# A squared-ReLU MLP's first matrix by a seven-product scheme: high and low rows of the stationary activations side by side in matmuls of 512 columns, two of four weight sums made by accumulating loads

## The chip, the cores and the metric

The kernel runs on one core of a Trainium2 chip. The metric is the device time of one launch in microseconds. The core's engines are TensorE (PE in the profile, its weight loads PEld), VectorE (DVE), ScalarE (ACT), GpSimd (POOL) and SyncE (SP, which here only issues DMAs). Each engine takes its instructions in its own fixed order; semaphores make it wait for others.

## What is computed

One layer of a hybrid decoder on 512 tokens, with 16 learned meta tokens ahead of them, all in float32: D_MODEL is 2048, D_FF 8192.

```python
u = rmsnorm(h, norm_mix[l])
proj = u @ w_in[l]
...
mix = jnp.concatenate([att.astype(x.dtype), hm], axis=-1)
h = h + mix @ w_out[l]
u = rmsnorm(h, norm_mlp[l])
h = h + jnp.square(jax.nn.relu(u @ w_up[l])) @ w_down[l]
```

The left-out part is a sliding-window attention with sinks and an mLSTM, both read from `proj` and concatenated. The change lies in `u @ w_up[l]`, which with its Relu and square is a matrix of 512 x 8192 results, each a sum over 2048.

## The kernel before

**Numbers.** A float32 product is made of three faster ones. `split` turns a tile into a high part, a cast to fp32r by ScalarE (L124), and a low part, source minus high part by VectorE (L125). Then high x high, high x low and low x high go into the same PSUM bank. Splitting a weight tile of 128 x 1024 takes one such pair of instructions; `hi_lo` gives the two result tiles, three pairs deep.

**Stages.** In order of time: w_in with attention and mLSTM, w_out (`tok_gemm`, L715 to L717), w_up (`up_quad`), w_down (L1104 to L1108). All four are matrix products against weights that stream in from DRAM once.

**w_up.** It is a Strassen-Winograd scheme: D_MODEL, D_FF and the tokens are each cut in halves or pairs, so that a block of results of 2 x 2 parts takes seven products in place of eight, at the price of sums of weights, of activations and of results. There are 32 quads (`NQ`), each of 256 columns of w_up: x11, x12, x21, x22 are its four weight parts of 128 x 1024 (eight k-tiles side by side), which come in two tiles `raws[0]` (x11, x12) and `raws[1]` (x22, x21) by two loads of 1 MB on SP's queue. Even quads use the two-deep pool of `raw_tile`, odd quads two tiles of their own, so four are there in all. The activations' operands y, seven pairs of high and low tiles, are split once and stay in SBUF.

The products p run in the order 0, 1, 5, 4, 6, 2, 3. The weight operands are x11, x12, s2, s1, s3, s4, x22, with s1 = x21 + x22, s2 = s1 - x11, s3 = x11 - x21, s4 = x12 - s2, all made by VectorE (`w_sum`, L753). A product is 8 k-tiles of three matmuls of 256 columns (L784: high weights on high rows, L785: high on low, L786: low on high), in which the weights are the 128 x 128 side that is loaded and the rows of y stream. Some of the sums over products are done in PSUM (a later product goes on in the bank X or Q without a start), the others by VectorE (L839, L848, L851) on copies that ScalarE made (L837, L840 and others). Results stand in `d` (two deep), which ScalarE takes through Relu (L849, L852, L853) and Square (L854). VectorE makes four more sums `fs` of d for w_down's own seven-product scheme (L857 to L860). Both go to DRAM by DMAs on ScalarE's queue (L861, L862).

**Quad 0** is different: its products lie between the last pieces of w_out, and its seven results stand in banks until VectorE joins them (L819 to L823).

**GpSimd** meanwhile does a job of its own: from quad 6 to 21 of the source, one unit of the residual `hd` a quad, in two halves; each half is a load into `res`, a product by a scalar and a store back (L1014, L1015, L1018). `res` is one tile, so each step waits for the last one. In w_down GpSimd issues the accumulating stores into `hd` (L1114).

**Order.** A tile framework's scheduler decides in which order each engine takes its instructions, from the program's order and from its own estimate of times; buffers come from pools, and an allocation waits for the release of the tile that had the place before.

## Time and profile before

| what | value |
|---|---|
| time, median of 3 runs | 1968.13 us (1967.82 to 1968.39) |
| the profiled execution's own time | 1967.29 us |
| its span in the trace | 1965.5 us |
| TensorE clock granted over the span | 0.998 |
| PE / VectorE / ScalarE / GpSimd busy | 99% / 71% / 51% / 12% |
| the w_up stage behind quad 0 | 733.5 to 1344.6 us |

The page gives busy times over the whole span; its slices of the span show PE at 9 tenths or more in all but the last one of 40, VectorE at 7 to 8 tenths from about 690 us on, and the DMA engines at 4 to 5 tenths in the w_up stage and 6 to 8 tenths in w_down. Instructions are listed with their line, the tile that they write and those that they read. A row of the list in order of time is: start, duration, engine, line, operation, and in brackets the idle time of the engine before it with what ended that. A row of the groups is: line, engine, operation, tiles, count, then busy time and mean duration in ns, then idle time before. PE busy is no sign of a limit by itself, as matmuls are pipelined: their durations overlap, and the distance of their starts is what one costs.

### The profile page before, as it was taken

The numbers are of one execution on the slowest core, as the hardware profiler recorded it, in microseconds if no ns is written. First come the engines' busy times: TensorE is split into PE (matmuls) and PEld (weight loads), VectorE is DVE, ScalarE is ACT, GpSimd is POOL, SyncE is SP. The second block draws the span as 40 slices with busy tenths as digits, with TensorE's granted clock in tenths as the row PEclk, the third lists the DMA queues.
The fourth block names the chain that finished last, engine by engine and source line by source line (L and its number), as shares of the span: only waits on it lengthen the run. The fifth ranks groups of instructions, "written<-read, shape, count | busy, mean of one in ns | idle before, by whom it ended". The sixth has DMA issues, their size and how long they took to land.

```text
span 1965.5 us, 30627 instructions
## 1 busy us (share of the span) xinstructions
PE 1948.6 (99%) x12240; PEld 1745.1 (89%) x12240; DVE 1405.3 (71%) x1843; ACT 1011.3 (51%) x1491; POOL 233.9 (12%) x346
## 2 busy tenths in 40 slices
PE   9999999999999999999999999999999999999997
PEld 7878889988888899999999999998888888888886
DVE  5547773233644378787878787878888988888888
ACT  4433542245533255555555555556566566655655
POOL 0112220011211001222222000001100010010001
PEclk9999999999999999999999999999999999999999
DMA  8412112221243335555555454547888887788866
GB/s 315 136 65 88 65 64 72 90 77 65 85 169 130 131 132 182 189 193 180 196 177 199 153 172 150 172 162 249 212 224 214 231 223 214 223 206 211 216 178 195
DMA packets 112752, 324.61 MB, mean 165 GB/s; under 512 B 14016, under 2 KB 50496, under 8 KB 93648
## 3 DMA queue, kind: packets, MB, share of 16 engines
q1 hardware_dynamic: 66880, 247.65, 36.9%
q0 software_dynamic: 12320, 41.95, 11.0%
q10 hardware_dynamic: 33408, 33.04, 5.3%
q8 instruction: 96, 1.57, 0.3%
q14 instruction: 48, 0.39, 0.1%
HBM read 244.45 MB, written 78.15 MB: 164 GB/s over the span
## 4 chain that ended last, share of the span: by engine, by line
PE 95%; DVE 2%; ACT 1%; issue 1%; POOL 0%; DMA 0%; DVEq 0%; ACTq 0%; POOLq 0%
PE g L171 10%; PE X L1107 6%; PE X L1108 6%; PE X L1104 6%; PE g L784 5%; PE g L786 5%; PE g L785 5%; PE a L784 5%; PE a L786 5%; PE a L785 5%; PE g L716 3%; PE g L715 3%; PE g L717 3%; PE Q L1107 3%; PE Q L1108 3%; PE Q L1104 3%
## 5 line engine op out<-in xcount | busy, mean ns | idle before, releaser
L124 ACT CAST whi<-raw 128x1024 fp32r<-128x1024 f32 x223 | 234.2, 1050 | 403.8 <-PE g L717 85.5
L125 DVE TENSOR_TENSOR wlo<-raw,whi 128x1024 fp32r<-128x1024 f32 x223 | 273.2, 1225 | 202.4 <-ACT whi L124 197.4
L125 DVE TENSOR_TENSOR wlo<-s,whi 128x1024 fp32r<-128x1024 f32 x255 | 311.9, 1224 | 108.2 <-ACT whi L124 106.9
L124 ACT CAST whi<-s 128x1024 fp32r<-128x1024 f32 x255 | 267.8, 1051 | 198.6 <-PE g L785 61.0
L171 PE MATMUL g<-s,whi 128*128 128x264 f32 x1216 | 205.0, 287 | 0.2 <-DVE qa L270 0.2
L171 PEld LDWEIGHTS g<-s,whi 128*128 128x128 f32 x1216 | 170.9, 189 | 5.4 <-issue 4.9
L1107 PE MATMUL X<-wlo,s 128*128 128x512 f32 x348 | 135.5, 389 | 0.1
L1108 PE MATMUL X<-whi,s 128*128 128x512 f32 x348 | 135.4, 389 | 0.0
L1104 PE MATMUL X<-whi,s 128*128 128x512 f32 x348 | 135.4, 389 | 0.0
L171 PE MATMUL g<-s,wlo 128*128 128x264 f32 x608 | 128.0, 287 | 0.0
L784 PE MATMUL a<-y,whi 128*128 128x256 f32 x448 | 125.6, 281 | 0.7 <-DVE d L839 0.7
L786 PE MATMUL a<-y,wlo 128*128 128x256 f32 x448 | 125.4, 280 | 0.6 <-DVE wlo L125 0.6
L785 PE MATMUL a<-s,whi 128*128 128x256 f32 x448 | 125.4, 280 | 0.0
L786 PE MATMUL a<-s,wlo 128*128 128x256 f32 x448 | 125.2, 279 | 0.0
L785 PE MATMUL a<-y,whi 128*128 128x256 f32 x448 | 125.2, 280 | 0.0
L784 PE MATMUL a<-s,whi 128*128 128x256 f32 x448 | 125.1, 279 | 0.0
L784 PE MATMUL g<-y,whi 128*128 128x256 f32 x444 | 124.6, 281 | 0.0
L785 PE MATMUL g<-s,whi 128*128 128x256 f32 x444 | 124.2, 280 | 0.0
L786 PE MATMUL g<-y,wlo 128*128 128x256 f32 x444 | 124.2, 280 | 0.0
L785 PE MATMUL g<-y,whi 128*128 128x256 f32 x444 | 124.1, 280 | 0.0
L786 PE MATMUL g<-s,wlo 128*128 128x256 f32 x444 | 124.0, 279 | 0.0
L784 PE MATMUL g<-s,whi 128*128 128x256 f32 x444 | 123.8, 279 | 0.0
(385 smaller groups left out, 5114.3 us busy)
## 6 DMA issues: line engine op xcount, KB each, us to landing
raw<-in_w_dram SPq DMA_DIRECT2D x144, 1024.0 KB, 5.1
rh<-in_w_dram SPq DMA_DIRECT2D x64, 512.0 KB, 5.6
hd<-c POOLq DMA_DIRECT2D x61, 512.0 KB, 5.6
fu<-fd SPq DMA_DIRECT2D x108, 256.0 KB, 3.9
fd<-d ACTq DMA_DIRECT2D x32, 512.0 KB, 3.2
fd<-fs ACTq DMA_DIRECT2D x31, 512.0 KB, 3.5
xtok<-in_x_dram SPq DMA_DIRECT2D x4, 1024.0 KB, 11.5
hs<-in_x_dram SPq DMA_DIRECT2D x16, 256.0 KB, 5.8
```

The lines of the kernel that those rows point to most:

```text
L124: act.copy(dst_hi, src)
L125: dve.tensor_tensor(out=dst_lo, in0=src, in1=dst_hi.bitcast(F32), op=ALU.subtract)
L171: pe.matmul(ps[s], w, x[:, PARTS[s]], start=first and kt == 0, stop=last and kt == KT - 1,)
L715: pe.matmul(ps[b][:], a, wh, start=kt == first, stop=False)
L716: pe.matmul(ps[b][:], a, wl, start=False, stop=False)
L717: pe.matmul(ps[b][:], c, wh, start=False, stop=kt == last)
L784: pe.matmul(out, wh, ah_, start=start and q == 0, stop=False, skip_group_check=True)
L785: pe.matmul(out, wh, al_, start=False, stop=False, skip_group_check=True)
L786: pe.matmul(out, wl, ah_, start=False, stop=q == KQ - 1, skip_group_check=True)
L1104: pe.matmul(out[:, t], a, wh[:, cols], start=start and h == q == 0, stop=False, skip_group_check=True)
L1107: pe.matmul(out[:, t], a, wl[:, cols], start=False, stop=False, skip_group_check=True)
L1108: pe.matmul(out[:, t], a2, wh[:, cols], start=False, stop=h == q == 1, skip_group_check=True)
```

## The change

**Rows.** The high and low rows of y are stored anew: for every k-tile the 256 high columns and right behind them the 256 low ones (`y_pair`, with `yy` the row of 512). In quads 1 to 31 a k-tile is now a matmul of 512 columns (high weights on the row) and one of 256 (low weights on the high half), in place of three of 256. PE's list of matmuls goes from 12096 to 10360 in the program. High x high and high x low thus come out in two halves of a whole bank and must be added: X, W and Q are banks of 512 columns now, `e` holds copies and PSUM sums of 512 columns (`accumulate`), and `join` adds the halves into `d`. Quad 0 keeps its matmuls of 256.

**Sums.** With signs turned, the operands are x11, x12, x11 + x21 + x22, x21 + x22, x11 + x21, x12 + x11 + x21 + x22, x22. Two sums are made by loads: `s0` gets x21 by a third load on SP and x11 on top of it by an accumulating load on GpSimd's queue; x21 gets x22 on top in the same way. VectorE makes the other two in place (x11 += x21, x12 += x11). The activations' sums turn signs to match, and the results' Relu becomes two instructions on alternate quarters of `d`, one with scale +1 and one with -1.

**Buffers.** Sum tiles go from three to two, `d` from two to one, the tile `shift` goes, `e` (128 x 2048 float32) comes, and both raw tiles are taken before the first load.

```diff
@@ -40,7 +40,7 @@
 QB = 2
 NQ = FF // P // 2
 HTOK = SEQ // 2
-NS_ = 3
+NS_ = 2
 FB = 5
 MAN = {mybir.EngineType.PE}
 ORDER = (0, 1, 5, 4, 6, 2, 3)
@@ -722,14 +722,15 @@
     b2s = ExitStack()
     b2 = b2s.enter_context(tc.tile_pool(name="b2", bufs=1, reuse_waits="tile"))
-    yh, yl = {}, {}
+    yy, yh, yl = {}, {}, {}
     def y_pair(p, j, t):
-        o = 16 * (j // 2)
-        yh[p, j], yl[p, j] = (t[:, o + i * 512 : o + (i + 1) * 512].rearrange("p (q n) -> p q n", q=2) for i in range(2))
-    b2.tile([P, 16], F32, name="shift")
+        o = 32 * (j // 3)
+        rows = t[:, o : o + 1024]
+        yy[p, j] = rows.rearrange("p (q m) -> p q m", q=2)
+        yh[p, j], yl[p, j] = (rows.rearrange("p (q a n) -> p a q n", q=2, a=2)[:, i] for i in range(2))
     for p in ORDER:
         for j in range(2):
             y_pair(p, j, b2.tile([P, 1024], F32R, name=f"y{p}_{j}"))
@@ -755,18 +756,19 @@
     done, summed = {}, {}
     def up_quad(quad):
-        raws = []
+        raws = [b2r.tile([P, 2048], F32, name=f"raw{i}") if quad % 2 else raw_tile() for i in range(2)]
         for i in range(2):
-            if quad % 2:
-                raw = b2r.tile([P, 2048], F32, name=f"raw{i}")
-            else:
-                raw = raw_tile()
-            load = sync.dma_start(out=raw[:], in_=io["w3"][quad, i])
+            load = sync.dma_start(out=raws[i][:], in_=io["w3"][quad, i])
             if quad == 2:
                 tc.keep_in_program_order(load)
-            raws.append(raw)
         x11, x12 = raws[0][:, :1024], raws[0][:, 1024:]
         x22, x21 = raws[1][:, :1024], raws[1][:, 1024:]
+        s0 = sum_tile()
+        if quad > 0:
+            sync.dma_start(out=s0[:], in_=io["w3"][quad, 1, :, 1024:])
+            pool.dma_start(out=s0[:], in_=io["w3"][quad, 0, :, :1024], accum_op=ALU.add)
+            pool.dma_start(out=x21, in_=io["w3"][quad, 1, :, :1024], accum_op=ALU.add)
         if quad == NQ - 1:
             u = sum_tile()
@@ -774,26 +776,32 @@
                 k = len(loaded)
                 loaded[k] = u[:, h * 512 : (h + 1) * 512]
                 load_unit(k, loaded[k])
-        s1, s2, s3, s4 = (sum_tile() for _ in range(4))
         nb = abank if quad % 2 else bank
-        def product(p, w, out, q0=0, q1=KQ, start=True):
-            for q in range(q0, q1):
-                wh, wl = (t[:, q * P : (q + 1) * P] for t in w)
-                ah_, al_ = yh[p, q // 2][:, q % 2], yl[p, q // 2][:, q % 2]
-                pe.matmul(out, wh, ah_, start=start and q == 0, stop=False, skip_group_check=True)
-                pe.matmul(out, wh, al_, start=False, stop=False, skip_group_check=True)
-                pe.matmul(out, wl, ah_, start=False, stop=q == KQ - 1, skip_group_check=True)
+        def relu(d, i):
+            r = d.rearrange("p (a b) n -> p b a n", a=2)[:, i]
+            act.activation(r, r, AF.Relu, scale=(1.0, -1.0)[i])
         if quad == 0:
...
             pa, pb, pc = (nb((P, 2, HTOK)) for _ in range(3))
             pd = nb((P, HTOK))
             pp2, pp6 = pd[:], pa[:, 1]
-            w_sum(s1, x21, x22, ALU.add)
-            w_sum(s2, s1[:], x11, ALU.subtract)
-            w_sum(s4, x12, s2[:], ALU.subtract)
-            early = [(p, operand(src), o) for p, src, o in ((0, x11, pa[:, 0]), (1, x12, pp2), (2, s4[:], pc[:, 1]))]
-            op4 = slot_operand(s1[:])
+            w_sum(s0, x21, x22, ALU.add)
+            w_sum(x21, x21, x11, ALU.add)
+            op0, op1 = operand(x11), operand(x12)
+            w_sum(x11, x11, s0[:], ALU.add)
+            w_sum(x12, x12, x11, ALU.add)
+            early = [(0, op0, pa[:, 0]), (1, op1, pp2), (2, operand(x12), pc[:, 1])]
+            op4 = slot_operand(s0[:])
             yield
             product(*early[0], 0, 2)
             yield
@@ -808,11 +816,10 @@
             product(4, op4, pb[:, 1])
             dve.tensor_tensor(out=w[1][:], in0=x22, in1=w[0][:].bitcast(F32), op=ALU.subtract)
             product(3, w, pc[:, 0])
-            w_sum(s3, x11, x21, ALU.subtract)
-            product(6, operand(s3[:]), pb[:, 0])
-            product(5, operand(s2[:]), pp6)
-            d = b2b.tile([P, 4, HTOK], F32, name="d", bufs=2)
+            product(6, operand(x21), pb[:, 0])
+            product(5, operand(x11), pp6)
+            d = b2b.tile([P, 4, HTOK], F32, name="d")
             v = b2b.tile([P, 4, HTOK], F32, name="fs")
             sb, u2, u = v[:, 2], v[:, 3], v[:, :2]
             act.copy(sb, pa[:, 0])
@@ -821,36 +828,49 @@
             dve.tensor_tensor(out=u, in0=v[:, 3:].to_broadcast([P, 2, HTOK]), in1=pb[:], op=ALU.add)
             dve.tensor_tensor(out=d[:, 3], in0=u[:, 0], in1=pb[:, 1], op=ALU.add)
             dve.tensor_tensor(out=d[:, 1:3], in0=u, in1=pc[:], op=ALU.add)
-            act.activation(d[:], d[:], AF.Relu)
         else:
-            X, B = nb((P, HTOK)), nb((P, 2, HTOK))
-            W, Q = B[:, 0], B[:, 1]
-            d = b2b.tile([P, 4, HTOK], F32, name="d", bufs=2)
-            product(0, operand(x11), X[:])
-            act.copy(d[:, 0], X[:])
-            w_sum(s1, x21, x22, ALU.add)
-            w_sum(s2, s1[:], x11, ALU.subtract)
+            def product(p, w, out, start=True):
+                for q in range(KQ):
+                    wh, wl = (t[:, q * P : (q + 1) * P] for t in w)
+                    row = yy[p, q // 2][:, q % 2]
+                    pe.matmul(out[:], wh, row, start=start and q == 0, stop=False, skip_group_check=True)
+                    pe.matmul(out[:, :HTOK], wl, row[:, :HTOK], start=False, stop=q == KQ - 1, skip_group_check=True)
+            def accumulate(dst, src, bank):
+                dve.tensor_tensor(out=dst, in0=src, in1=bank[:], op=ALU.add)
+            def join(d, e):
+                dve.tensor_tensor(out=d, in0=e[..., :HTOK], in1=e[..., HTOK:], op=ALU.add)
+            X, W, Q = (nb() for _ in range(3))
+            e = b2b.tile([P, 4, 512], F32, name="e")
+            d = b2b.tile([P, 4, HTOK], F32, name="d")
+            product(0, operand(x11), X)
+            act.copy(e[:, 0], X[:])
             product(1, operand(x12), W)
+            w_sum(x11, x11, x21, ALU.add)
             if quad == NQ - 1:
                 for k in (2, 3):
                     split_unit(k, loaded[k])
-            product(5, operand(s2[:]), X[:], start=False)
-            dve.tensor_tensor(out=d[:, 0], in0=d[:, 0], in1=W, op=ALU.add)
-            act.copy(d[:, 2], X[:])
-            product(4, operand(s1[:]), Q)
-            w_sum(s3, x11, x21, ALU.subtract)
-            act.copy(d[:, 1], Q)
-            product(6, operand(s3[:]), X[:], start=False)
-            w_sum(s4, x12, s2[:], ALU.subtract)
-            act.copy(d[:, 3], X[:])
-            product(2, operand(s4[:]), Q, start=False)
-            dve.tensor_tensor(out=d[:, 3], in0=d[:, 3], in1=d[:, 1], op=ALU.add)
-            act.activation(d[:, 0], d[:, 0], AF.Relu)
-            product(3, operand(x22), X[:], start=False)
-            dve.tensor_tensor(out=d[:, 2], in0=d[:, 2], in1=Q, op=ALU.add)
-            act.activation(d[:, 2:4], d[:, 2:4], AF.Relu)
-            act.activation(d[:, 1], X[:], AF.Relu)
+            product(5, operand(x11), X, start=False)
+            accumulate(e[:, 0], e[:, 0], W)
+            act.copy(e[:, 2], X[:])
+            product(4, operand(x21), Q)
+            act.copy(e[:, 1], Q[:])
+            join(d[:, 0], e[:, 0])
+            product(6, operand(s0[:]), X, start=False)
+            w_sum(x12, x12, x11, ALU.add)
+            accumulate(e[:, 3], e[:, 1], X)
+            product(2, operand(x12), Q, start=False)
+            accumulate(e[:, 2], e[:, 2], Q)
+            product(3, operand(x22), X, start=False)
+            join(d[:, 2:4], e[:, 2:4])
+            act.copy(e[:, 1], X[:])
+            join(d[:, 1], e[:, 1])
+        relu(d[:], 0)
+        relu(d[:], 1)
         done[quad] = act.activation(d[:], d[:], AF.Square)
         fs = b2b.tile([P, 4, HTOK], F32, name="fs")
         summer = dve if quad < NQ - 1 else pool
@@ -931,9 +951,10 @@
             split(yh[0, j][:], yl[0, j][:], y11)
             split(yh[1, j][:], yl[1, j][:], y21)
             split(yh[2, j][:], yl[2, j][:], y22)
-            dve.tensor_tensor(out=t1, in0=y12, in1=y11, op=ALU.subtract)
-            dve.tensor_tensor(out=t2, in0=y22, in1=t1, op=ALU.subtract)
-            dve.tensor_tensor(out=t4, in0=y21, in1=t2, op=ALU.subtract)
+            dve.tensor_tensor(out=t1, in0=y11, in1=y12, op=ALU.subtract)
+            dve.scalar_tensor_tensor(out=t2, in0=y22, scalar=-1.0, in1=t1, op0=ALU.mult, op1=ALU.subtract)
+            dve.scalar_tensor_tensor(out=t4, in0=t2, scalar=-1.0, in1=y21, op0=ALU.mult, op1=ALU.subtract)
             dve.tensor_tensor(out=t3, in0=y22, in1=y12, op=ALU.subtract)
             for p, src in ((4, t1), (3, t4), (6, t3), (5, t2)):
                 split(yh[p, j][:], yl[p, j][:], src)
```

The places in the order, first VectorE between quad 0 and quad 1. Names: `fs_66..` and `g_63..` are quad 0's results, `d_6613` its output, raw0 and raw1 quad 1's weights, wlo the low half of an operand; L125 is the subtraction of `split`. Before:

```order
L125 TENSOR_TENSOR wlo_6642<-raw0_6630,whi_6641 128x1024
L125 TENSOR_TENSOR wlo_6673<-raw0_6630,whi_6672 128x1024
L819 TENSOR_TENSOR d_6613<-fs_6614,g_6349 128x256
L820 TENSOR_TENSOR fs_6614<-fs_6614,g_6346 128x256
L753 TENSOR_TENSOR s_6634<-raw1_6632 128x1024
L821 TENSOR_TENSOR fs_6614<-fs_6614,g_6347 128x512
```

After, at the same place (`d_6609` is quad 0's output, `raw0_6627` quad 1's first tile):

```order
L826 TENSOR_TENSOR d_6609<-fs_6610,g_6345 128x256
L827 TENSOR_TENSOR fs_6610<-fs_6610,g_6342 128x256
L828 TENSOR_TENSOR fs_6610<-fs_6610,g_6343 128x512
L125 TENSOR_TENSOR wlo_6641<-raw0_6627,whi_6640 128x1024
L829 TENSOR_TENSOR d_6609<-fs_6610,g_6343 128x256
L830 TENSOR_TENSOR d_6609<-fs_6610,g_6344 128x512
L125 TENSOR_TENSOR wlo_6662<-raw0_6627,whi_6661 128x1024
L877 TENSOR_TENSOR fs_6620<-d_6609 128x256
L879 TENSOR_TENSOR fs_6620<-d_6609 128x256
L878 TENSOR_TENSOR fs_6620<-fs_6620,d_6609 128x256
L880 TENSOR_TENSOR fs_6620<-d_6609,fs_6620 128x256
L754 TENSOR_TENSOR raw0_6627<-raw0_6627,raw1_6628 128x1024
```

Both low halves of quad 1's first products stood ahead of quad 0's result sums; now three of those stand ahead of the first low half, five ahead of the second, and quad 0's four fs sums stand ahead of quad 1's first weight sum.

Second, GpSimd's queue in the middle of w_up, the residual loop. Two halves of it before:

```order
L1014 DMA res_9920<-hd2_0_5097 128x256
L1015 TENSOR_SCALAR res_9920<-res_9920,i2_6500 128x256
L1018 DMA hd2_0_5097<-res_9920 128x256
L1014 DMA res_9924<-hd2_0_5097 128x256
L1015 TENSOR_SCALAR res_9924<-res_9924,i2_6500 128x256
L1018 DMA hd2_0_5097<-res_9924 128x256
```

The same two halves after (`s_8807` and `raw1_8804` are s0 and x21 of a coming quad):

```order
L1035 DMA res_9161<-hd2_0_5097 128x256
L1036 TENSOR_SCALAR res_9161<-res_9161,i2_6497 128x256
L1039 DMA hd2_0_5097<-res_9161 128x256
L770 DMA s_8807<-in_w3_dram 128x1024
L1035 DMA res_9165<-hd2_0_5097 128x256
L771 DMA raw1_8804<-in_w3_dram 128x1024
L1036 TENSOR_SCALAR res_9165<-res_9165,i2_6497 128x256
L1039 DMA hd2_0_5097<-res_9165 128x256
```

The two accumulating loads of a quad stand among the residual's steps, one ahead of the second half's load and one ahead of its product.

Third, VectorE in a steady quad after the change (`e_8448` and `d_8449` are the running quad's, `raw_8620` and `raw_8621` the next quad's weights):

```order
L125 TENSOR_TENSOR wlo_8580<-raw1_8438,whi_8579 128x1024
L841 TENSOR_TENSOR e_8448<-e_8448,a_8445 128x512
L125 TENSOR_TENSOR wlo_8634<-raw_8620,whi_8633 128x1024
L754 TENSOR_TENSOR raw_8620<-raw_8620,raw_8621 128x1024
L841 TENSOR_TENSOR e_8448<-e_8448,a_8447 128x512
L125 TENSOR_TENSOR wlo_8655<-raw_8620,whi_8654 128x1024
L844 TENSOR_TENSOR d_8449<-e_8448 128x512
L754 TENSOR_TENSOR raw_8620<-raw_8620 128x1024
```

The next quad's first weight sum (the first L754, which reads the accumulated x21 in `raw_8621`) now stands between two PSUM sums of the running quad, and the join into the one `d` stands ahead of the next quad's second weight sum.

7 lines of the change are left out of this document (added).

## Prediction

> **What bounds the kernel now.** I read the page, then busy time by stretch, then single matmuls in order of time, then groups, waits and DMA of the w_up stage.
>
> ```profile
> span 1965.5 us, 30627 instructions
> PE 1948.6 (99%) x12240; PEld 1745.1 (89%) x12240; DVE 1405.3 (71%) x1843; ACT 1011.3 (51%) x1491; POOL 233.9 (12%) x346
> PE 95%; DVE 2%; ACT 1%; issue 1%; POOL 0%; DMA 0%; DVEq 0%; ACTq 0%; POOLq 0%
> ```
>
> TensorE carries 95% of the chain that ended last. A busy PE says little by itself, since matmuls overlap, so I look at the stages.
>
> ```profile
> core 0: us, PE busy (x) PEld busy (x) DVE busy (x) ACT busy (x) POOL busy (x), PEclk, DMA share, GB/s
> 733.50:1344.60 611.10, 609.79 (x5179) 609.37 (x5179) 483.21 (x566) 334.12 (x469) 77.52 (x104) 1.00 0.53 178
> 1000.00:1100.00 100.00, 100.00 (x853) 100.00 (x851) 78.95 (x92) 54.81 (x77) 19.95 (x26) 1.00 0.54 182
> 1500.00:1600.00 100.00, 100.00 (x443) 82.81 (x442) 88.29 (x88) 61.87 (x72) 7.77 (x9) 1.00 0.83 220
> ```
>
> The second row is the w_up stage. PE never rests there, at full clock; VectorE has 21% free, ScalarE 45%, the DMA engines 46%. So this stage is as long as its matmuls. What one costs is the distance between starts, not its latency of 280 or 389 ns:
>
> ```profile
> 1011.04 0.28 PE L784 MATMUL a<-y,whi 128*128 128x256 f32 x1
> 1022.82 0.28 PE L785 MATMUL a<-y,whi 128*128 128x256 f32 x1
> 1699.66 0.39 PE L1104 MATMUL X<-whi,s 128*128 128x512 f32 x1
> 1711.90 0.39 PE L1104 MATMUL X<-whi,r 128*128 128x512 f32 x1
> 324.51 11.50 PE g L171 x95
> ```
>
> Between the first two rows lie 100 steps: 117.8 ns each. Between the next two, 54 steps: 226.7 ns. The line through both is 8.9 ns + 0.425 ns a column; the last row (264 columns, 11.50 us / 95 = 121.1 ns) lies on it. So a matmul has about 8.9 ns of its own, whatever its width.
>
> **The change part by part.** *The pairs.* In each of 31 quads, 7 products of 8 k-tiles lose one matmul: 31 x 56 = 1736. Columns stay equal (512 + 256 for 3 x 256). The gain is 1736 x 8.9 ns = **-15.5 us**. A quad goes from 168 x 117.8 = 19.79 us to 56 x (226.7 + 117.8) = 19.29 us, a product from 2.83 to 2.76 us. No row shows 512 and 256 columns in turn; the ends are 0 (the pair gains nothing) and -15.5 us, and I take the latter, since three widths lie on one line.
>
> The Trainium skill (TensorE: Matmul & The Clock Gate, section "Wait — 56ns, not 53.3ns?") puts the fixed cost of a warm matmul at about 2.5 ns. By it the pairs would give 1736 x 2.5 = 4.3 us; the trace's 8.9 ns does not agree, and I go by the trace.
>
> *VectorE and ScalarE in a quad.*
>
> ```profile
> L125 DVE TENSOR_TENSOR wlo<-s,whi 128x1024 fp32r<-128x1024 f32 x124 | 151.7, 1225 | 66.0 <-ACT whi L124 65.0
> L753 DVE TENSOR_TENSOR s<-raw 128x1024 f32<-128x1024 f32 x45 | 54.7, 1216 | 0.0
> L857 DVE TENSOR_TENSOR fs<-d 128x256 f32<-128x256 f32 x31 | 13.5, 434 | 4.6 <-ACT d L854 4.6
> L823 DVE TENSOR_TENSOR d<-fs,g 128x512 f32<-128x512 f32 x1 | 0.7, 681 | 0.0
> L124 ACT CAST whi<-s 128x1024 fp32r<-128x1024 f32 x124 | 129.9, 1050 | 122.6 <-PE g L785 61.0 <-PE a L785 58.3 <-DVE s L753 0.6
> L852 ACT ACTIVATE d<-d 128x512 f32<-128x512 f32 x31 | 19.4, 627 | 0.1
> L840 ACT COPY d<-g 128x256 f32<-128x256 f32 x15 | 5.5, 364 | 0.0
> ```
>
> VectorE: 7 low halves x 1.225, 2 sums (were 4) x 1.216, 3 PSUM adds of 512 columns x 0.681, one join of 512 x 0.681, two joins and four fs sums of 256 x 0.434: 8.6 + 2.4 + 2.0 + 0.7 + 2.6 = 16.3 us; before it was 8.6 + 4.9 + 1.3 (three adds of 256) + 1.7 = 16.5. That is 85% of 19.29 us. ScalarE: its 54.81% of 19.79 is 10.8 us; four PSUM copies double in width (at most 0.627 for 0.364), and the Relus stay within 0.2 us: under 12 us, 62%. Both fit, so I cost them at nothing. The cover is the three hi/lo buffers: a cast starts when the product three before it ends, which leaves two products (5.5 us) for cast and subtraction; without it each us late is a us of PE.
>
> *Start of quad 1.* The rows of the order show the low half of quad 1's first product now behind three adds of quad 0's results.
>
> ```profile
> 729.70 0.28 PE L784 MATMUL a<-y,whi 128*128 128x256 f32 x1
> 737.51 0.38 PE L786 MATMUL a<-y,wlo 128*128 128x256 f32 x1 [0.58 <-DVE wlo L125]
> 729.90 0.37 ACT L818 COPY fs<-g 128x256 f32<-128x256 f32 x1 [1.90 <-PE g L786]
> ```
>
> Before, quad 1 begins at 729.70 straight behind quad 0, and its third product stands until 737.51. After, the copy of 729.90 comes first; two adds of about 0.35 and one of 0.6 (rows overlap by 0.08) end at 731.6, the low half at 732.8. Product two follows 2.76 us behind product one, ending at 738.1. VectorE meanwhile waits for quad 0's square (to 735.9), then has four fs sums (1.4), two weight sums (2.3), one add (0.6) and the low half (1.2): 741.4. Against 737.5 that is 3.9, and 0.2 for the shorter products already counted: **+4.1 us** (ends 0 and 6, were the first accumulated weights late too).
>
> *End of the stage.* The last square now waits for a PSUM copy, a join and two Relus in place of one Relu.
>
> ```profile
> 1344.52 0.39 ACT L853 ACTIVATE d<-a 128x256 f32<-128x256 f32 x1 [1.42 <-PE a L786]
> 1346.63 1.05 ACT L124 CAST whi<-rh 128x1024 fp32r<-128x1024 f32 x1 [0.63 <-ACT d L854]
> 1355.64 0.50 PE X L1107
> ```
>
> The cast at 1346.63 stands behind it on ScalarE, and the chain from there reaches PE at 1355.64, already 0.3 us late. Copy 0.6, join 0.4, Relu 0.6 for Relu 0.39: **+1.3 us** (ends 0 and 1.3).
>
> *Loads in place of sums.* Per quad: one more load of 512 KB on SP and two accumulating loads of 512 KB on GpSimd.
>
> ```profile
> raw<-in_w_dram SPq DMA_DIRECT2D x144, 1024.0 KB, 5.1
> hd<-c POOLq DMA_DIRECT2D x61, 512.0 KB, 5.6
> fd<-d ACTq DMA_DIRECT2D x32, 512.0 KB, 3.2
> q1 hardware_dynamic: 24884, 79.43, 48.7%
> q0 software_dynamic: 7606, 27.68, 32.2%
> q10 hardware_dynamic: 10560, 10.49, 16.4%
> ```
>
> No accumulation into SBUF is in the trace; the nearest is hd<-c (into DRAM). The q1 and q0 rows are of 1400 to 1900 us: 243 us of all engines for 79.43 MB, 3.07 us a MB, and 161 us for 27.68 MB, 5.82 us a MB. The q10 row is of 1100 to 1300 us: 3.13 us a MB. A quad now needs 6.4 (weights) + 3.3 (d, fs) = 9.7 us of the engines, and will need 1.6 + 6.1 more: 17.4 of 19.29 us, 90%. That still fits, against 83% in the third stage, where PE doesn't rest either.
>
> Is an accumulated weight in time? x22 is split, and its buffer free, 13.4 us into a quad (four products and cast and subtraction). The sum that needs the accumulated x21 two quads later stands 16.3 us into the quad between: 19.29 + 2.9 = 22.2 us. It takes up to 7 us for the load (behind its 1 MB neighbour; 5.1 is the median), 0.9 to issue and 5.6 to land: 13.5. So about 9 us are spare, and I cost it at 0 while GpSimd issues at once. The Trainium skill (DMA: Bandwidth & Descriptors, section "Anatomy of one DMA — SWDGE (gpsimd) path") fits 2.0 us + bytes / 436 GB/s, 3.2 us for 512 KB, an estimate; the 5.6 us of the row is longer, and by the page 2.4 us more would be spare.
>
> *Sum:* -15.5 + 4.1 + 1.3 = -10.1 us. The profiled execution took 1967.29 us (span 1965.5 and 1.8 around it), so 1957.2; the median of the runs is 0.84 above it: **1958.0 us**.
>
> **The rivals.** *A: GpSimd's queue becomes the bound (slower).* Until now GpSimd rescales 32 halves of the residual there, each a load, a product and a store, each waiting for the one before.
>
> ```profile
> 784.40 0.59 POOL L1014 DMA_DIRECT2D res<-hd  x1 [3.53 <-DMA hd<-res]
> 1054.74 0.54 POOL L1014 DMA_DIRECT2D res<-hd  x1 [1.82 <-DMA hd<-res]
> 1063.41 1.46 POOL L1015 TENSOR_SCALAR res<-res,i 128x256 f32<-128x256 f32 x1 [8.13 <-DMA res<-hd]
> 1070.34 0.71 POOL L1015 TENSOR_SCALAR res<-res,i 128x256 f32<-128x256 f32 x1 [2.10 <-DMA res<-hd]
> 1074.47 0.54 POOL L1014 DMA_DIRECT2D res<-hd  x1 [2.52 <-DMA hd<-res]
> L1014 POOL DMA_DIRECT2D res<-hd x32 | 17.3, 540 | 112.7 <-DMA hd<-res 112.7
> L1015 POOL TENSOR_SCALAR res<-res,i 128x256 f32<-128x256 f32 x32 | 35.0, 1095 | 110.6 <-DMA res<-hd 110.6
> L1114 POOL DMA_DIRECT2D hd<-c x60 | 51.7, 864 | 515.9 <-DVE c L1111 483.0 <-ACT c L1120 26.9 <-DVE s L1073 3.1
> ```
>
> Thirty halves took 290 us: 19.34 us for two, and nobody waited. Now two halves stand in the queue between one quad's accumulated weight and the next's, for 15 quads, so the loop must keep 19.29 us. The issues (0.86) hide in waits, but the waits (112.7 and 110.6 us, 3.6 us each) grow, as accumulations stand ahead in the same queue and the engines are fuller. The bounds are 0 and 3.05 us (an accumulation's engine time) for each of the two transfers behind one. Loss = 15 x (loop - 19.29) - 9 us: it starts at 19.9 us and eats the gain at 20.6. With 1 us for each of the two the loop is 21.3: +21 us, 1979; with 3.05, 25.4: +83 us. For it: the loop has no spare on average and DMA goes to 90% and more. Against it: single waits range from 2.1 to 8.1 us and last while a weight burst is in flight, so the loop shifts to the gaps and falls in with the quad's period, as it did towards the end, where two halves took 19.7 us (1054.74 to 1074.47), about a quad.
>
> *B: the single d buffer.* The join of the next quad's d stands on VectorE until d has been stored. The store is issued 7.4 us into that quad, the join's turn is at 9 us and PE notices from about 12 us. With 3.2 us to land nothing is lost; with 5.6 us, as 512 KB takes among the fuller traffic of stage three, about 1 us late in every other quad: 15 us, 1973; half of that and it is a draw, which I take as its time: about 1966.
>
> *C: the fixed cost is not the matmul's.* If the weight load that each matmul brings sets it, or unlike widths in turn cost more, the pairs give little: 0 to 4 us, and +4.1 + 1.3 is left: 1969. Against it stand the three widths on one line. The skill's 2.5 ns named above would give 1968 to 1970 as well; the trace speaks against it.
>
> **How the numbers follow.** Forecast 0.45, A 0.35, B 0.14, C 0.06. 0.2% is about 3.9 us, what a measurement can tell: faster is below 1964.2, slower above 1972.1. The forecast is nearly all faster (0.43 of 0.45); of A, loops below 20.4 us leave a gain (0.05), to 20.9 a draw (0.06), the rest is slower (0.24); B gives 0.02 faster, 0.07 same, 0.05 slower; C 0.04 same, 0.02 slower. With the 0.02 of the forecast, that is 0.50 faster, 0.19 same, 0.31 slower. The low end is the sum without the costs at start and end, 1968.1 - 15.5, and 1 us for the stall that quad 1 has already: 1951.5. The high end is a loop of 21.5 us, 15 x 2.2 - 9 - 10.1 = +14: 1982; beyond it I leave about 0.12.
>
> **What would show it.** Right: matmul steps of 226.7 and 117.8 ns in turn, quads of 19.3 us, PE waiting about 1.5 us longer than now in all at 730 to 742 and at the end of the stage, and no idle PE between. A shows as VectorE waiting at the weight sum for a DMA from GpSimd's queue, quads of 20 us and more between quads 8 and 21, and normal ones behind. B shows as VectorE waiting at the join of d for the store; C as steps above these. It is wrong if the w_up stage without its first quad isn't about 15 us shorter.

## The result and the profile after

The changed kernel takes 2018.56 us (median of 4 runs, 2013.93 to 2021.05) against 1967.97 before: 1.0254 times as long, 95% interval 1.0235 to 1.0273. The forecast was 1958.0 with a range to 1982.0, so it is wrong in sign and outside its range. Below, every run has its median and, in brackets, its ratio to the kernel before that was measured beside it, with the 95% interval of that ratio. One execution of before_32 took 4861.73 us, two and a half times the others, and stands in no ratio. The profiled execution took 2017.66 us with a span of 2015.9, 50.4 more than before.

The page of the changed kernel, and two of its DMA rows (name, queue, count, size, median us from issue to landing):

```profile
span 2015.9 us, 27502 instructions
PE 1965.9 (98%) x10504; PEld 1672.6 (83%) x10504; DVE 1396.7 (69%) x1874; ACT 1028.8 (51%) x1461; POOL 289.3 (14%) x408
L838 PE MATMUL a<-y,wlo 128*128 128x256 f32 x448 | 128.4, 287 | 13.8 <-DVE wlo L125 13.7
L844 DVE TENSOR_TENSOR d<-e 128x256 f32<-128x256 f32 (+1 forms) x93 | 47.9, 515 | 81.1 <-DMA fd<-d 81.0
fd<-d ACTq DMA_DIRECT2D x32, 512.0 KB, 6.1
raw<-in_w_dram POOLq DMA_DIRECT2D x31, 512.0 KB, 6.4
```

PE has 1736 matmuls fewer and is still busy 17.3 us longer: the gain was meant to show here and doesn't. PE now waits for low halves, VectorE for the store of `d`. The w_up stage in stretches (columns: busy us and count of PE, PEld, VectorE, ScalarE, GpSimd, then the granted clock, the DMA engines' share, GB/s):

```profile
700.00:750.00 50.00, 45.01 (x282) 39.90 (x281) 35.61 (x46) 25.27 (x40) 6.58 (x9) 0.93 0.68 195
800.00:850.00 50.00, 50.00 (x285) 43.40 (x285) 39.40 (x51) 30.23 (x40) 15.57 (x18) 1.00 0.85 240
1050.00:1100.00 50.00, 44.09 (x228) 38.06 (x229) 33.09 (x42) 22.62 (x29) 12.24 (x17) 0.90 0.80 235
1250.00:1300.00 50.00, 50.00 (x285) 43.34 (x284) 37.42 (x48) 28.98 (x37) 4.33 (x5) 1.00 0.81 219
```

Three things are to be seen. From 700 to 750 us and in the middle of the stage PE stands still, and where it did, the clock of that stretch is below 1. The DMA engines are at 80% and more; the forecast had 90%. And in the last stretch PE never waits and yet issues 285 matmuls in 50 us, 175 ns each, where the forecast had 172. What one pair costs, and where the quads lie, in starts of matmuls:

```profile
1239.88 0.40 PE L837 MATMUL g<-s,whi 128*128 128x512 f32 x1
1242.00 0.40 PE L837 MATMUL g<-y,whi 128*128 128x512 f32 x1
732.08 0.50 PE L837 MATMUL a<-y,whi 128*128 128x512 f32 x1 [1.45 <-ACT whi L124]
838.30 0.40 PE L837 MATMUL g<-y,whi 128*128 128x512 f32 x1
1168.19 0.39 PE L837 MATMUL a<-y,whi 128*128 128x512 f32 x1
1365.27 0.40 PE L837 MATMUL a<-y,whi 128*128 128x512 f32 x1
1386.69 0.40 PE L1125 MATMUL X<-whi,s 128*128 128x512 f32 x1
```

Between the first two lie six pairs: 353 ns each, and a quad of 56 pairs takes 19.77 us where nothing stops it. That is what three matmuls of 256 columns took before (3 x 117.8 = 353). So the whole forecast gain is missing in every quad. The other rows are the first matmuls of quad 1, of two quads 15 apart, of the last quad and of w_down. Quad 1 ends at 759.35; before the change w_down began at 1344.26. With them the 50.4 us split up:

| part | us |
|---|---|
| quad 1 begins at 732.08, was 729.70 | +2.4 |
| quad 1: 27.27 us; stops in the whole stage before were 614.56 - 31 x 19.77 = 1.8 | 7.5 - 1.8 = +5.7 |
| 15 quads from 838.30 to 1168.19: 329.9 for 296.5 | +33.4 |
| the last quad: 21.42 | +1.7 |
| other quads, four of which are 0.1 to 0.3 short | -0.8 |
| from w_down's first matmul to the end: 629.2, was 621.2 | +8.0 |

Who waits in the stage, by the view of waits (engine, tile, line, what it waits for: us in all, times, longest):

```profile
POOL res L1036 <- DMA res<-hd: 123.9, 30, 6.0
POOL res L1035 <- DMA hd<-res: 105.4, 31, 7.3
DVE d L844 <- DMA fd<-d: 81.0, 30, 7.7
DVE raw L754 <- DMA raw<-in_w_dram: 27.1, 6, 5.6
PE a L838 <- DVE wlo L125: 13.7, 10, 4.1
```

Both rivals with a mechanism are there: VectorE waits at the weight sum (L754) for an accumulated weight, rival A, and at the join (L844) for the store of `d`, rival B. One of the quads in order of time, GpSimd first, then VectorE, then PE:

```profile
1013.70 0.55 POOL L1035 DMA_DIRECT2D res<-hd  x1 [6.15 <-DMA hd<-res]
1018.99 0.94 POOL L770 DMA_DIRECT2D s<-in_w_dram  x1
1021.41 0.91 POOL L771 DMA_DIRECT2D raw<-in_w_dram  x1
1028.12 0.69 POOL L1036 TENSOR_SCALAR res<-res,i 128x256 f32<-128x256 f32 x1 [5.80 <-DMA res<-hd]
1035.69 0.54 POOL L1035 DMA_DIRECT2D res<-hd  x1 [5.99 <-DMA hd<-res]
1033.77 1.23 DVE L754 TENSOR_TENSOR raw<-raw,raw 128x1024 f32<-128x1024 f32 x1 [5.30 <-DMA raw<-in_w_dram]
1036.78 0.39 PE L838 MATMUL a<-y,wlo 128*128 128x256 f32 x1 [2.05 <-DVE wlo L125]
```

Two halves of the residual take 1035.69 - 1013.70 = 22 us (the second half's load, at 1020.86, is not shown), and one quad's two accumulating loads stand among them. The load into x21, issued at 1021.41, has landed when the sum starts at 1033.77, 12 us later. VectorE has waited 5.3 us by then, and PE 2.05. The waits at L754 and L844 overlap and cause each other, so these rows don't tell what each one costs; the experiments do.

### The profile page after: what moved, and what is told of

The parts are those of the page before. It is cut to its first block, busy times and chain, and to the rows that moved or that the text cites. A ratio compares the mean times of both kernels' runs of the same rounds, so it can differ in the third digit from the quotient of the medians.

```text
span 2015.9 us, 27502 instructions
## 1 busy us (share of the span) xinstructions
PE 1965.9 (98%) x10504; PEld 1672.6 (83%) x10504; DVE 1396.7 (69%) x1874; ACT 1028.8 (51%) x1461; POOL 289.3 (14%) x408
## 5 line engine op out<-in xcount | busy, mean ns | idle before, releaser
L124 ACT CAST whi<-raw 128x1024 fp32r<-128x1024 f32 x319 | 335.3, 1052 | 551.3 <-PE a L837 106.7
L125 DVE TENSOR_TENSOR wlo<-raw,whi 128x1024 fp32r<-128x1024 f32 x319 | 390.2, 1228 | 188.7 <-ACT whi L124 183.8
L125 DVE TENSOR_TENSOR wlo<-s,whi 128x1024 fp32r<-128x1024 f32 x159 | 194.4, 1223 | 45.5 <-ACT whi L124 45.5
L124 ACT CAST whi<-s 128x1024 fp32r<-128x1024 f32 x159 | 167.1, 1051 | 72.5 <-PE Q L1129 25.1
L837 PE MATMUL a<-y,whi 128*128 128x512 f32 x448 | 165.7, 404 | 9.7 <-ACT whi L124 4.6
L837 PE MATMUL a<-s,whi 128*128 128x512 f32 x448 | 166.1, 404 | 0.0
L837 PE MATMUL g<-s,whi 128*128 128x512 f32 x420 | 154.3, 401 | 0.0
L837 PE MATMUL g<-y,whi 128*128 128x512 f32 x420 | 152.6, 400 | 1.2 <-DVE e L841 1.0
L837 PEld LDWEIGHTS a<-y,whi 128*128 128x128 f32 x448 | 84.9, 191 | 31.1 <-ACT whi L124 5.9
L844 DVE TENSOR_TENSOR d<-e 128x256 f32<-128x256 f32 (+1 forms) x93 | 47.9, 515 | 81.1 <-DMA fd<-d 81.0
L837 PEld LDWEIGHTS a<-s,whi 128*128 128x128 f32 x448 | 85.9, 192 | 21.3
```

Of the source, the lines that this page charges most:

```text
L124: act.copy(dst_hi, src)
L125: dve.tensor_tensor(out=dst_lo, in0=src, in1=dst_hi.bitcast(F32), op=ALU.subtract)
L837: pe.matmul(out[:], wh, row, start=start and q == 0, stop=False, skip_group_check=True)
L844: dve.tensor_tensor(out=d, in0=e[..., :HTOK], in1=e[..., HTOK:], op=ALU.add)
```

## The experiments

My theory after the result had three parts. A: GpSimd's queue costs most of the 33.4 us. B: the store of the single `d` costs the rest there or most of it (these two are each other's rivals). P: a matmul's cost depends on where its rows lie in SBUF, and the change, which moved the rows of y by 64 bytes against the weights, lost in this way what the pairs won; the rival is that the pairs are worth nothing.

**no_res** is the changed kernel without the residual's rescaling.

```diff
-            if 6 <= quad < 6 + NJ * NB:
+            if False:
```

> The changed kernel without GpSimd's rescaling of the residual in w_up (left out, so 32 loads, products and stores of 128 x 256 are not done). Theory A (the residual loop in GpSimd's queue, 22.4 us for two halves from 812 to 1126 us, makes the accumulated x21 late): the five waits of VectorE at the first weight sum for the weights' DMA (4.87, 5.39, 5.16, 5.30, 5.64 us) go, with them most of the 33 us that the quads from 838 to 1168 us take over 19.77 us each: about 1986 us. Theory B (the store of the one d buffer is what stops PE): these waits at the join stay as long as they are (3 to 7 us) and at most 15 us are won: 2003 or more. Both: quads that are not disturbed stay at 19.77 us, as the pairs give nothing.

Measured: 1985.32 us (1.0088, 1.0072 to 1.0103). One stretch of the stage:

```profile
860.00:1160.00 300.00, 300.00 (x1702) 260.33 (x1701) 229.24 (x288) 171.13 (x215) 26.79 (x31) 1.00 0.84 237
```

PE doesn't stop once in these 300 us, in which it had stopped in most quads. VectorE still waits 61.5 us at the join, up to 3.9 us at a time until the last quad, and that costs nothing. Theory A, to 1 us; but the run can't say whether the queue or the traffic did it, since both are gone. What is left over the kernel before, 17.7 us, lies outside these quads.

**d0_two** gives `d`'s first quarter a tile of its own, two deep.

```diff
-            d = b2b.tile([P, 4, HTOK], F32, name="d")
+            dr = b2b.tile([P, 3, HTOK], F32, name="d")
+            d0 = b2b.tile([P, HTOK], F32, name="d0", bufs=2)
...
```

The store and the Square become two instructions each, one for each tile, and the Relus three.

> The changed kernel with d's first quarter in a tile of its own, two deep, so that the first join of a quad no longer waits for the store of d; the other three quarters stay one deep, their first join comes some 7 us later in the quad. Theory B: the 81 us of VectorE's waits at the join go, and PE's losses in the quads at 838, 859, 1031 and 1061 us with them: 15 to 25 us, about 1997. Theory A: the waits at the weight sum stay (five of about 5 us) and cost what they cost now, only the two losses of 1.2 us at 855 and 873 us and some 5 us behind them go: 2008 to 2015.

Measured: 2015.52 us (1.0246, 1.0229 to 1.0264). The waits at the join are gone from the view of waits, and this row is there:

```profile
DVE raw L754 <- DMA raw<-in_w_dram: 50.4, 13, 6.7
```

13 waits at the weight sum in place of 6. Taking B's wait away alone brings 3 us, which is within the runs' own spread of 7 us: VectorE then waits for GpSimd's queue.

**dve_sums** has the two sums back on VectorE.

```diff
-            sync.dma_start(out=s0[:], in_=io["w3"][quad, 1, :, 1024:])
-            pool.dma_start(out=s0[:], in_=io["w3"][quad, 0, :, :1024], accum_op=ALU.add)
-            pool.dma_start(out=x21, in_=io["w3"][quad, 1, :, :1024], accum_op=ALU.add)
+            w_sum(s0, x21, x11, ALU.add)
+            w_sum(x21, x21, x22, ALU.add)
```

> The changed kernel with the two weight sums back on VectorE (s0 = x21 + x11 and x21 += x22 by two more additions of 128 x 1024) in place of the third load and the two accumulating loads. DMA is then as before the change, and so is GpSimd's residual loop. VectorE has 16.3 + 2.4 = 18.7 us of work in a quad of 19.77 us. Theory A: no wait for weights is left, 1985 us, the losses at the start of quad 1, at the end of the stage and in w_down's start stay. Rival: with 95% VectorE becomes the bound, PE waits for low halves in every quad, 20.3 us or more a quad: over 2000 us.

Measured: 2014.17 us (1.0243, 1.0227 to 1.0259), the rival. No stop is long, but there is one of 1 to 2.4 us in most quads, at the product whose low half is late:

```profile
860.00:1160.00 300.00, 286.60 (x1600) 244.15 (x1599) 255.69 (x300) 162.00 (x200) 58.12 (x72) 1.00 0.49 170
```

Quads take 20.35 to 22.0 us. VectorE is busy 85%, not 95%, so it is late rather than full. Theory A had left no wait for weights, but there is one: in nineteen quads VectorE stands at a weight sum for a plain weight load, 15.0 us in all. One of them:

```profile
904.62 1.23 DVE L754 TENSOR_TENSOR s<-raw 128x1024 f32<-128x1024 f32 x1 [1.20 <-DMA raw<-in_w_dram]
```

So pairs without the accumulating loads don't pay here either. How much the order costs by itself, no run tells.

**split512** issues each matmul of 512 columns as two of 256.

```diff
-                    pe.matmul(out[:], wh, row, start=start and q == 0, stop=False, skip_group_check=True)
+                    pe.matmul(out[:, :HTOK], wh, row[:, :HTOK], start=start and q == 0, stop=False, skip_group_check=True)
+                    pe.matmul(out[:, HTOK:], wh, row[:, HTOK:], start=start and q == 0, stop=False, skip_group_check=True)
```

> The changed kernel with each matmul of 512 columns issued as two of 256 (high weights on the high half, then on the low half of the row, into the two halves of the same bank), all else the same. If the pairs are worth nothing where PE runs steadily (three of 256 took 353.4 us/1000 before, 512 and 256 take 353.0 in steady quads): undisturbed quads stay at 19.8 us and the time within 4 us of the changed kernel, 2015 to 2022. If the pairs are worth the 8.9 ns a matmul and something else in the changed kernel eats it: quads of 20.3 us, 15 us slower, 2033.

(Two starts in one bank change the first k-tile's part of the sum; count, shape and order of the matmuls are as said.) Measured: 2014.25 us (1.0237, 1.0221 to 1.0252). The first matmuls of two quads that lie eight apart:

```profile
1178.14 0.28 PE L837 MATMUL g<-y,whi 128*128 128x256 f32 x1
1339.42 0.28 PE L837 MATMUL g<-y,whi 128*128 128x256 f32 x1
```

A quad takes 161.28 / 8 = 20.16 us, 168 matmuls of 120.0 ns. Neither expectation fits as a whole: the time stayed, as the first one said, since in this kernel fewer quads stop while every quad is longer; but the quads are those of the second one. So the pairs are worth 20.16 - 19.77 = 0.39 us a quad, 12 us in all, and something else in the changed kernel costs 0.39 us more than before. In the unchanged list of quad 0, too, matmuls of 256 columns go at 120.0 ns after the change and at 117.5 to 118 before; there only the place and the layout of y have changed.

**before_aligned** is the kernel before with the place of y alone changed.

```diff
-        o = 16 * (j // 2)
+        o = 32 * (j // 3)
...
-    b2.tile([P, 16], F32, name="shift")
```

> The kernel before, with only the place of the y tiles changed: no shift tile and the changed kernel's offset in the slots, so that y starts where it starts after the change; matmuls of 256 columns as before. Theory P: 120.0 ns a matmul and 20.16 us a quad as in split512, 31 x 0.38 us more: about 1980 us. Rival (the place is of no weight): 117.8 ns, 19.78 us and 1968 us.

Measured: 1979.96 us (1.0062, 1.0046 to 1.0078), on the theory's number. Two quads, 20 apart, in this kernel:

```profile
769.65 0.28 PE L783 MATMUL a<-y,whi 128*128 128x256 f32 x1
1172.85 0.28 PE L783 MATMUL a<-y,whi 128*128 128x256 f32 x1
```

403.20 / 20 = 20.16 us. An offset of 64 bytes in SBUF costs 12 us, with the layout of y and the matmuls as before. (Tiles taken behind y may move along with it; PE reads none of them in these quads.) This is what the pairs' gain was paid with.

**whole_res** rescales the residual in whole units.

```diff
-                for half in range(2):
-                    cols = slice(half * HTOK, (half + 1) * HTOK)
-                    res = b2b.tile([P, HTOK], F32, name="res")
-                    pool.dma_start(out=res[:], in_=hd[j][b // 2][:, b % 2, cols])
+                res = b2b.tile([P, 512], F32, name="res", tag="eu")
+                pool.dma_start(out=res[:], in_=hd[j][b // 2][:, b % 2])
...
```

> The changed kernel with the residual rescaled in whole units of 128 x 512: one load, product and store a quad in GpSimd's queue in place of two of each, the same bytes. Theory A (it is the number of steps that wait for one another in GpSimd's queue): one half's loop takes about 11 us of the 22.4, a whole unit's 11 to 14 us, below the 19.77 us of a quad, so the accumulated weights are in time as without the residual, about 1986 us. Rival (the residual's traffic delays the weights, not the queue): the bytes stay, so the waits of about 5 us at the weight sum stay, 2010 us or more.

Measured: 2014.51 us (1.0241, 1.0222 to 1.0259), against theory A, as it seems. Rows of GpSimd show why that doesn't follow:

```profile
946.95 0.94 POOL L770 DMA_DIRECT2D s<-in_w_dram  x1
949.00 0.56 POOL L1033 DMA_DIRECT2D res<-hd  x1 [1.12 <-DMA hd<-res]
967.51 0.54 POOL L1033 DMA_DIRECT2D res<-hd  x1 [7.65 <-issue]
973.16 0.94 POOL L770 DMA_DIRECT2D s<-in_w_dram  x1
```

The scheduler had put two units (two loads of `res`, L1033) between one quad's accumulating load into s0 (L770) and the next's, in eight quads instead of sixteen: 26.2 us here, for a quad of 19.77. The kernel didn't do what the experiment was for, and it was made again as paced.

**shifted** is whole_res with y at its old offset.

```diff
-        o = 32 * (j // 3)
+        o = 16 * (j // 2)
...
+    b2.tile([P, 16], F32, name="shift")
```

> whole_res with the rows of y put 64 bytes further on, at the offsets against the weight tiles that y had before the change (the shift tile and its place in the slots back). Theory P (the place of the moving rows against the weights sets what a matmul costs: three of 256 columns took 353.2 ns before and 360.0 in split512, with nothing changed in the matmuls but where they read and write): undisturbed quads leave 19.77 us; if the gain of a pair at the new place, 7.0 ns, holds at the old one, they take 346 ns a pair and 19.4 us, 12 us less than whole_res. Rival (the place is of no weight, the split matmuls cost more since they write to two halves of a bank): 19.77 us and the time of whole_res.

Measured: 2010.71 us (1.0221, 1.0205 to 1.0237). Undisturbed quads take 19.70 us (1107.54 to 1343.92 us, twelve quads): they do leave 19.77, but not for 19.4. At this offset a pair is worth 0.07 us a quad, not 0.39. So place and pairing don't add up: what y's place saves on matmuls of 256 columns it doesn't save on the pair.

**grouped_w** is whole_res with a product's eight matmuls of 512 columns first.

```diff
                 for q in range(KQ):
-                    wh, wl = (t[:, q * P : (q + 1) * P] for t in w)
+                    wh, row = w[0][:, q * P : (q + 1) * P], yy[p, q // 2][:, q % 2]
...
+                for q in range(KQ):
+                    wl, row = w[1][:, q * P : (q + 1) * P], yy[p, q // 2][:, q % 2]
...
```

> whole_res with the eight matmuls of 512 columns of a product first and its eight of 256 behind them, in place of one and one in turn. Theory C (unlike widths in turn cost more): the 512s go at 226.7 ns as in w_out and w_down, the 256s at 117.8 to 120.0, a product at 2.76 to 2.77 us and a quad at 19.3 to 19.4 us, 12 us less than whole_res. Rival (a limit of 0.46 ns a column in this stage, whatever the order): 236 and 117 ns go on, 19.77 us a quad and the time of whole_res.

Measured: 2013.38 us (1.0219, 1.0176 to 1.0262), not clearly less than whole_res, since larger stops (3.6 to 7 us each) ate it. Undisturbed quads take 19.53 us; the matmuls of 256 go at 119 ns on average, those of 512 at 230 (226 to 236). At 226.7 and 120.0 a quad would be 19.4. So grouping takes away 0.24 of the 0.36 us that a quad is longer than that, and the rest is there without the turn of widths. But pairs in turn go at 19.43 us a quad too, at times (see below), so the turn alone does not explain the 0.36.

**paced** puts one whole unit between the accumulating loads of one quad and the next.

```diff
-            pool.dma_start(out=x21, in_=io["w3"][quad, 1, :, :1024], accum_op=ALU.add)
+            accs[quad] = pool.dma_start(out=x21, in_=io["w3"][quad, 1, :, :1024], accum_op=ALU.add)
...
+                with tc.issue_after(accs[quad].ins):
...
```

> whole_res with one residual unit between one quad's accumulating loads and the next's (whole_res had two: the order of GpSimd's queue put the 16 units into 8 quads, 2 x 11.8 us each, above a quad's 19.77). Theory A (the steps of the queue): 11.8 us and the two issues fit in 19.77 us, so no wait at the weight sum is left and the time is that of the run without the residual, 1985 us. Rival (the residual's traffic): the bytes a quad are those of the changed kernel, the waits of about 5 us stay in several quads, over 2000 us. What the changed kernel loses at the start of quad 1 and at the end of the stage stays in both.

Measured: 1992.2 us (1.0126, 1.0105 to 1.0146). No wait at the weight sum for a DMA is left behind quad 1; so it was the queue, not the bytes. But four quads take 20.7, 24.3, 21.4 and 20.3 us, and the waits say for what:

```profile
DVE d L844 <- DMA fd<-d: 67.5, 28, 6.6
```

**paced_grouped** is paced with the matmuls of grouped_w.

> paced with the eight matmuls of 512 columns of a product ahead of its eight of 256. Theory P: in grouped_w undisturbed quads took 19.53 us (12.13 + 4.63 + 2.77); 31 x 0.24 us = 7 us less than paced, about 1978 us if paced comes to 1985. Rival: a product whose low half is not due until its ninth matmul gives VectorE slack too, so that less is lost at the start of quad 1 as well, 1973 us.

Measured: 1996.55 us (1.0137, 1.0114 to 1.0159). Undisturbed quads are at 19.53 us, but there are four stops of 2.3 to 7 us, three behind the join and one behind the weight sum. Both expectations failed: the 0.24 us a quad are there, and the stops cost more than they bring. Whether grouping would pay with B gone was not run.

**before_32** is the kernel before with y 32 bytes away in place of 64.

```diff
-        o = 16 * (j // 2)
+        o = (0, 0, 8, 24)[j]
...
-    b2.tile([P, 16], F32, name="shift")
+    b2.tile([P, 8], F32, name="shift")
```

> The kernel before, with y 32 bytes from the weights' offset in place of 64 (a shift tile of 8 numbers, and the slots' offsets to match). At 0 a matmul took 120.0 ns, at 64 bytes 117.8. Theory P: the step depends on how far apart the two lie; between the two, 118 to 120 ns, 1970 to 1980 us, if it falls off with the distance; 117.8 ns and 1968 us if any other place but 0 will do. Rival (place is of no weight and the 12 us came from something else in that kernel): 1968 us, with another pattern of steps than in the kernel before excluded.

Measured: 1965.07 us, 0.9988 of the kernel before (0.9978 to 0.9997); nine of its ten runs lie from 1964.47 to 1965.58. Quads 20 apart:

```profile
768.47 0.28 PE L784 MATMUL a<-y,whi 128*128 128x256 f32 x1
1162.33 0.28 PE L784 MATMUL a<-y,whi 128*128 128x256 f32 x1
```

393.86 / 20 = 19.69 us, 117.2 ns a matmul: below both other places, so it doesn't fall off with distance, as one expectation had it. It is the only version here that beats the kernel before.

**d0_paced** is paced and d0_two together.

> paced and d0_two together: one residual unit a quad in GpSimd's queue, and d's first quarter two deep. Theory (the queue and the single d are the whole loss in the middle of the stage): paced's quads of 20.7, 24.3 and 21.4 us, in which VectorE waited 4 to 6.6 us at the join for the store of d, fall to 19.77 as well, 7 us less than paced: 1985 us, 17.5 above the kernel before, which are the start of quad 1 and the end of the stage. Rival (fuller DMA engines make some load late whatever waits for it): other waits take the place of these, 1990 us or more.

Measured: 1984.53 us (1.0084, 1.0067 to 1.0101), as the theory had it.

```profile
860.00:1160.00 300.00, 300.00 (x1701) 260.42 (x1700) 232.96 (x288) 178.34 (x245) 61.82 (x76) 1.00 0.88 265
```

With all of the residual's bytes, and the DMA engines at 88%, PE doesn't stop. So queue and single `d` together are the whole loss in the middle.

**d0_paced_32** has y 32 bytes away as well.

```diff
-        o = 32 * (j // 3)
+        o = (0, 0, 8, 24)[j]
...
+    b2.tile([P, 8], F32, name="shift")
```

> d0_paced with the rows of y 32 bytes from the weights' offset, the place at which three matmuls of 256 columns took 351.6 ns in before_32. Theory P: if a pair is worth 7 ns there too, 345 ns and 19.3 us a quad, 14 us less than d0_paced. Rival: as at 64 bytes in shifted (19.70 us) the pair is worth nothing away from offset 0: 19.7 us a quad, 2 us less than d0_paced.

Measured: 1977.0 us (1.0045, 1.0030 to 1.0060), 7.5 less than d0_paced, between the two expectations. Quads 20 apart:

```profile
800.29 0.39 PE L838 MATMUL g<-y,whi 128*128 128x512 f32 x1
1189.76 0.39 PE L838 MATMUL g<-y,whi 128*128 128x512 f32 x1
```

389.47 / 20 = 19.47 us. The quads by place of y against the weights and by matmul (us; at 64 bytes a quarter of the rows lies 64 to the other side, at 32 likewise):

| y against the weights | three of 256 | 512 and 256 | pairs worth |
|---|---|---|---|
| 0 bytes | 20.16 | 19.77 | 0.39 |
| 32 bytes | 19.69 | 19.47 | 0.22 |
| 64 bytes | 19.77 | 19.70 | 0.07 |

The kernel before stands at 64 bytes on the left, the change at 0 on the right: equal by chance.

## Why the prediction was wrong

**The pairs: -15.5 us forecast, 0 measured.** The step that failed is "the line through both is 8.9 ns + 0.425 ns a column". Its points were taken in stages whose rows lie at different places: w_up at 64 bytes, w_down at 0, w_in at several (worked out from the sizes of the kernel's tiles; the traces hold no addresses). As the place alone moves the point of 256 columns between 117.2 and 120.0 ns, the third width's lying on the line said little. At one place, 0 bytes, the pairs do bring something: 20.16 - 19.77 = 0.39 us a quad, 12.1 us in all, 7 ns for each matmul saved in place of 8.9. But y had been moved to that place, and this cost 12.2 us (before_aligned). The line of the diff that changes the offset I read as a matter of layout and gave no cost. That the two are equal is chance.

What a matmul costs by itself stays open. At 0 bytes 256 columns take 120.0 ns (split512, before_aligned) and 512 take 226.7 (w_down): 0.417 ns a column and 13.3 ns a matmul. The Trainium skill (TensorE: Matmul & The Clock Gate, section "Wait — 56ns, not 53.3ns?") has about 2.5 ns for the latter; these runs don't agree. By that line a pair is 346.7 ns and a quad 19.4 us, and some quads go so: one behind a stop (19.43 us at 1168.19), and in no_res one (818.20 to 837.63) with no stop since quad 1. Most are at 19.77. Rival C named unlike widths in turn as a cause; grouped_w takes away two thirds of the missing 0.36 us a quad, but since pairs in turn reach 19.43 as well, this doesn't show that the turn is the cause.

**Start and end: +5.4 forecast, +17.8 measured** (2.4 + 5.7 + 1.7 + 8.0). The path of the low halves was right at the start. But the loss began earlier than I had it, at ScalarE: its copy of quad 0's result, which waits for PE, stands ahead of the casts of quad 1's weights, so the casts start at 730.98 and were at 724.37 before. Rows of ScalarE, VectorE and PE at the start, and of VectorE, ScalarE and PE at the end of the stage:

```profile
730.98 2.00 ACT L124 CAST whi<-raw 128x1024 fp32r<-128x1024 f32 x2
732.51 1.22 DVE L125 TENSOR_TENSOR wlo<-raw,whi 128x1024 fp32r<-128x1024 f32 x1
741.59 0.66 PE L837 MATMUL a<-y,whi 128*128 128x512 f32 x1 [2.37 <-ACT whi L124]
743.51 0.58 PE L838 MATMUL a<-y,wlo 128*128 128x256 f32 x1 [0.18 <-DVE wlo L125]
1386.54 2.35 DVE L1094 TENSOR_TENSOR s<-raw 128x1024 f32<-128x1024 f32 x2
1388.81 0.42 DVE L844 TENSOR_TENSOR d<-e 128x256 f32<-128x256 f32 x1
1391.58 1.05 ACT L124 CAST whi<-rh 128x1024 fp32r<-128x1024 f32 x1 [0.59 <-ACT d L874]
1404.92 0.63 PE L1125 MATMUL X<-whi,s 128*128 128x512 f32 x1
1405.34 0.63 PE L1128 MATMUL X<-wlo,s 128*128 128x512 f32 x1
```

The low half of quad 1's first product ended at 733.7, forecast 732.8. That of its third product was there at 743.5, forecast 741.4: quad 0's square ended 1.0 us later than I had it, and the first weight sum waited 0.7 us for an accumulated weight. What I left out follows: PE's clock. After the stop PE runs at half speed for some microseconds (0.93 over that stretch of 50 us, so 3.5 us lost). At the end the join stands behind two weight sums of w_down (2.35 us), which I had not looked for; the cast that I had 1.3 us late starts 4.9 us behind w_down's first matmul, and was 2.4 behind it before. Then PE waits again and goes at half speed: 0.42 us from start to start for 512 columns in the last two rows, in place of 0.227. No run took these costs away; they are read from the rows. It fits that d0_paced, which loses nothing in the middle, is still 16.6 us above the kernel before.

**Accumulating loads: 0 forecast, +33.4 measured.** This is rival A, with a chance of 0.35, and rival B in its shadow: pacing the queue (paced) takes 26.4 us off the changed kernel, and d's first quarter two deep on top of that (d0_paced) 7.7 more. The step that failed is "I cost it at 0 while GpSimd issues at once". A's mechanism, its condition (the loop above 19.9 us) and the quads in which it shows were right; the bounds (19.34 to 25.4 us) held the loop's 22.4. The choice of 21.3 was low, and the 9 us of spare were spent sooner: the accumulating load took 12 us there, not 6.5. (The Trainium skill's formula of DMA: Bandwidth & Descriptors, section "Anatomy of one DMA — SWDGE (gpsimd) path", gives an estimate of 3.2 us for 512 KB; no accumulating load here was below 5.3.) By the prediction's own formula a loop of 22.4 and a quad of 19.77 make 15 x 2.6 - 9 = 30 us. That this comes so near is in part luck, as that formula has only waits in it. The row of these fifteen quads:

```profile
838.30:1168.19 329.89, 307.36 (x1683) 262.55 (x1681) 229.16 (x287) 169.48 (x211) 92.02 (x114) 0.97 0.80 237
```

PE was idle for 22.5 us of them. Behind four of the stops the granted clock was 0.50, for 17.1 us in all, nearly all of them busy: that makes some 8 us more. What I weighed wrongly is the chance: the loop had no spare on average, and the argument that it would fall in with the quad's period came from one instance.

**The single d buffer, rival B:** 6 to 8 us once A is gone (paced against d0_paced: 7.7 us in the medians, 5.9 in the profiled executions), 0 without the residual (no_res). The store took 6.1 us to land in the median, where I had 3.2 to 5.6. I had 8 us for B and rightly put it behind A; with A in place it is hidden.

**What was right:** VectorE and ScalarE carried their new work (no stop of PE in d0_paced's middle), and the DMA engines at 80 to 90% were enough.

## What to carry to other kernels

Measure a matmul's cost at the very place in SBUF at which it will run, before and after an edit that moves a tile: here 64 bytes cost as much as the merging of 1736 matmuls had won. Before work is put into a queue that holds a chain of waiting steps, add up the chain's loop per period; if it has no spare, the new work is late by the difference, every period. And look at how a scheduler has filled the queue before an experiment on it is believed.

## What the runs showed of the hardware

- The place of the moving rows against the weight tiles changes a matmul's step: for 256 columns 120.0 ns at 0 bytes, 117.2 at 32, 117.8 at 64. The mechanism was not found. As only y was moved, no run tells either whether its place against the weights counts or its place by itself.
- At 0 bytes the pair has two speeds: 347 ns, and 353 on average in a pattern that repeats every three pairs. The faster one was seen behind a stop (after, from 1160 us) and, in no_res from 813 us, without one; in both it passed into the slower one within about two quads. What turns the one into the other stays open.
- A stop of PE costs more than its length. One of 2.4 us (946.81 to 949.18) was followed by half clock; a row of PE, and the stretch behind it with its granted clock of 0.57:

```profile
949.18 0.39 PE L838 MATMUL a<-y,wlo 128*128 128x256 f32 x1 [1.97 <-DVE wlo L125]
950.00:954.00 4.00, 4.00 (x14) 3.27 (x13) 3.96 (x5) 2.76 (x5) 3.10 (x3) 0.57 0.09 32
```

  The Trainium skill (TensorE: Matmul & The Clock Gate, section "What's actually happening") has the clock halved after an idle window of about 3.4 us; here less was enough, and of the stops of 2 us and more not all were followed by it.
- An accumulating load of 512 KB into SBUF took 5.3 us from issue to landing at best, 6.4 in the median and 13.3 at worst (the 31 into x21 in the changed kernel; those into s0: 5.5, 7.4 and 11.1).
